# Hybrid encoder layer: the last layer norm taken during the last three expert units, their tokens normed apart

## Chip, cores and metric

The kernel runs on one core of a Trainium2 chip. The metric is device time in microseconds (us) of one execution, the median of several. Engines are named as the profile names them: PE (matrix products), DVE, ACT and POOL (elementwise work; POOL also issues transfers, among them all indirect ones), SP (issues transfers only). Sixteen DMA engines move the data of all issuing engines. Each engine runs its own instructions strictly in the order in which they stand.

## What is computed

A token-mixing sub-layer (sparse attention beside a convolution branch), then a mixture of experts, each with a residual and a layer norm. The change touches the end of the second sub-layer, for 512 prompt tokens and 64 sample tokens (576 rows of 1024 floats):

```
h2 = x * (1 + sc2) + sh2
# top-1 group, top-2 of its 4 experts: every token has two of 16 experts
act = silu(gate) * up * combine[:, :, None]
y = einsum('nef,efd->nd', act, w_down)
x = layer_norm(ALPHA * x + (1 + g2) * y, ln2_g, ln2_b)
```

## The kernel before

The first 690 us or so are the dense part: modulation products (`adap`, weights `wada`), the input projection (`acc`, weights split into a high and a low part by ACT L139 and DVE L140), attention, convolution, output projection, first norm, routing. A scheduler orders this part by its own timing model. The first modulation products need `wada` loads from SP's queue; `hh` and `hl`, the inputs of every `acc` product, need those.

Two rows of DRAM scratch stand for each token in `z_scr`: rows 0 to 575 begin as the residual, rows 576 to 1151 as a broadcast row (L416, one 2304 KB copy from DRAM to DRAM that POOL issues; L418 does the same for `h2_scr`). A token's first expert adds its result to the token's first row, the second expert to its second row, so z = row t + row 576 + t is what the last norm takes.

The experts run in thirteen units, an order written out by hand on PE, DVE and ACT (`manual_schedule`). Units 0 to 3 are four fixed experts; units 4, 8, 10 and 12 hold one expert with up to 128 tokens; units 5 and 6 one expert in two blocks; units 7, 9 and 11 two small experts with up to 64 tokens each. For each block POOL gathers the tokens' rows (L1119, `xg`), PE transposes them (L1134), multiplies by gate and up weights (`pg`), ACT and DVE make `hm`, PE turns it (`pht`) and ACT copies it (`hT`, L1166). The down product (`pd`; L1182, or L1186 for two experts) of one unit stands between the steps of the next unit: `product(p)` makes the row of gates `yo` on ACT and DVE (L1172, L1173), multiplies it with `pd` (L1193), and POOL adds the rows to `z_scr` (`add_rows`, L1194: an indirect transfer that accumulates, called a scatter below). Weights come into a ring of four slots through SP's queue; expert j's slot is free for expert j + 4, and the last weight loads are issued in the time of unit 9's product.

After the last unit all engines read a flag for overflowing experts (L1492, L1494); a loop would handle those and runs zero times here. The last unit's scatter is issued behind that. Then, for five tiles of 128 (the last 64) tokens: SP loads both rows of each token (`zt`, L1525), DVE adds them (L1527), tile 0 takes its statistics on DVE and the others on ACT (L1515, L1517, L1518), DVE applies them with gain and bias (`rows3`; L1529, L1530), and SP stores to y (L1531).

## Time and profile before

| what | value |
|---|---|
| median of 3 runs | 878.06 us (875.38 to 880.29) |
| the profiled execution | 880.75 us |
| its span (first to last instruction) | 879.1 us |
| PE, DVE, ACT, POOL busy | 90%, 74%, 41%, 15% of the span |
| clock granted to PE over the span | 0.95 of full |

The span is counted from the first instruction's time; the profiled execution's own time is 1.65 us longer than the span. A time such as "at 840.92" is microseconds from the span's start in the profiled execution. A row of the timeline gives start, duration, engine, line and operation, and in brackets how long the engine stood idle before it and what released it.

### The profile page before, as it was taken

How to read it: one execution, taken by the hardware profiler on the slowest of the kernel's cores; microseconds unless marked ns; L12 is line 12 of the kernel's file. 1: busy time of each engine (PE TensorE's matmuls, PEld its weight loads, DVE VectorE, ACT ScalarE, POOL GpSimd, SP SyncE). 2: the span in 40 equal slices, each digit the busy share in tenths (PEclk: the TensorE clock that was granted, in tenths of full speed). 3: DMA queues.
4: the chain of work that ended last, by engine and by line, in shares of the span. 5: the costliest groups of instructions: out<-in, count | busy, mean ns of one | idle time of the engine just before them, and what ended most of it. 6: DMA issues, size and time to landing. Idle time of an engine off the chain costs nothing.

```text
span 879.1 us, 13265 instructions
## 1 busy us (share of the span) xinstructions
PE 792.4 (90%) x4827; PEld 641.6 (73%) x4827; DVE 647.6 (74%) x1275; ACT 358.5 (41%) x654; POOL 132.3 (15%) x169
## 2 busy tenths in 40 slices
PE   4899999999999999999999999899938999999910
PEld 3788888887878879879899799888826676645400
DVE  1569999989999889988896425428896896655337
ACT  3243141324344335547733852312433664334304
POOL 2300000310100000000100001020347342221100
PEclk9999999999999999999999999899957999999965
DMA  9998663482423224232443106585695999699345
GB/s 295 343 340 261 195 213 119 122 241 54 149 71 95 76 75 113 89 100 84 129 118 113 39 1 228 188 259 213 197 329 139 345 366 310 199 363 373 97 164 169
DMA packets 101202, 162.06 MB, mean 184 GB/s; under 512 B 9667, under 2 KB 67163, under 8 KB 101137
## 3 DMA queue, kind: packets, MB, share of 16 engines
q1 hardware_dynamic: 87104, 122.74, 42.3%
q0 software_dynamic: 12688, 34.26, 14.5%
q10 hardware_dynamic: 1344, 4.22, 1.3%
q8 instruction: 38, 0.62, 0.3%
q14 instruction: 28, 0.22, 0.1%
HBM read 146.01 MB, written 26.13 MB: 196 GB/s over the span
## 4 chain that ended last, share of the span: by engine, by line
PE 60%; DVE 7%; DMA 4%; issue 2%; ACT 1%; POOL 1%; POOLq 0%; DVEq 0%; ACTq 0%
PE acc L242 7%; PE acc L244 7%; PE acc L243 7%; PE pd L1182 5%; PE pdot L528 3%; PE pg L1152 2%; PE pg L144 2%; DMA wraw<-in_w_att_out_dram 2%; PE pg L146 2%; PE pg L145 2%; PE tm L144 2%; PE tm L146 2%; PE tm L145 2%; PE pl L652 2%; PE po L660 2%
## 5 line engine op out<-in xcount | busy, mean ns | idle before, releaser
L588 DVE SCALAR_TENSOR_TENSOR y<-ue,dwT,y 128x604 f32<-128x604 f32 (+17 forms) x232 | 183.3, 828 | 1.9 <-ACT y L586 1.6
L242 PE MATMUL acc<-hh,wlo 128*128 128x288 f32 (+1 forms) x504 | 152.9, 304 | 1.3 <-DVE wlo L140 1.3
L243 PE MATMUL acc<-hh,whi 128*128 128x288 f32 (+1 forms) x504 | 150.6, 299 | 0.0
L244 PE MATMUL acc<-hl,whi 128*128 128x288 f32 (+1 forms) x504 | 149.4, 300 | 0.0
L139 ACT CAST whi<-wraw 128x1024 fp32r<-128x1024 f32 (+1 forms) x72 | 75.1, 1044 | 175.2 <-PE acc L244 83.1
L140 DVE TENSOR_TENSOR wlo<-wraw,whi 128x1024 fp32r<-128x1024 f32 (+1 forms) x72 | 87.4, 1214 | 53.6 <-ACT whi L139 53.3
L242 PEld LDWEIGHTS acc<-hh,wlo 128*128 128x128 f32 (+1 forms) x504 | 94.4, 187 | 17.2 <-issue 8.8
L243 PEld LDWEIGHTS acc<-hh,whi 128*128 128x128 f32 (+1 forms) x504 | 94.4, 187 | 5.2 <-issue 5.1
L244 PEld LDWEIGHTS acc<-hl,whi 128*128 128x128 f32 (+1 forms) x504 | 93.7, 187 | 5.5 <-issue 5.2
L144 PE MATMUL tm<-wlo,hh 128*128 128x512 f32 x128 | 50.5, 397 | 0.4 <-DVE wlo L140 0.4
L145 PE MATMUL tm<-whi,hh 128*128 128x512 f32 x128 | 50.4, 394 | 0.0
L146 PE MATMUL tm<-whi,hl 128*128 128x512 f32 x128 | 49.8, 391 | 0.0
L140 DVE TENSOR_TENSOR wlo<-ring,whi 128x1024 fp32r<-128x1024 f32 x30 | 36.4, 1222 | 17.7 <-ACT whi L139 15.0
L1182 PE MATMUL pd<-ring,hT 128*128 128x512 f32 x96 | 44.0, 601 | 1.2 <-ACT hT L1166 1.2
L139 ACT CAST whi<-ring 128x1024 fp32r<-128x1024 f32 x30 | 31.3, 1048 | 31.2 <-PE pg L146 27.4
L242 PE MATMUL acc<-oh,wlo 128*128 128x288 f32 x128 | 39.7, 310 | 4.5 <-DVE gt L744 4.0
L244 PE MATMUL acc<-yl,whi 128*128 128x288 f32 x128 | 39.3, 310 | 0.6 <-DVE yl L721 0.5
L244 PE MATMUL acc<-ol,whi 128*128 128x288 f32 x128 | 39.3, 310 | 0.0
L243 PE MATMUL acc<-oh,whi 128*128 128x288 f32 x128 | 39.2, 307 | 0.0
L243 PE MATMUL acc<-yh,whi 128*128 128x288 f32 x128 | 38.3, 301 | 0.0
L242 PE MATMUL acc<-yh,wlo 128*128 128x288 f32 x128 | 37.9, 297 | 0.0
L1194 POOL DMA_INDIRECT z_scr<-yo,idt x13 | 22.3, 1712 | 83.2 <-DVE yo L1193 74.4
(482 smaller groups left out, 1773.5 us busy)
## 6 DMA issues: line engine op xcount, KB each, us to landing
ring<-in_w_gate_up_dram SPq DMA_DIRECT2D x62, 512.0 KB
wraw<-in_w_in_dram SPq DMA_DIRECT2D x48, 512.0 KB
wada<-in_w_ada_dram SPq DMA_DIRECT2D x32, 512.0 KB
ring<-in_w_down_dram SPq DMA_DIRECT2D x32, 512.0 KB
wada<-in_w_ada_dram SPq DMA_DIRECT2D x32, 256.0 KB
gates_scr<-glg POOLq DMA_DIRECT2D x16, 288.0 KB
gt<-gates_scr POOLq DMA_DIRECT2D x16, 288.0 KB
wraw<-in_w_conv_out_dram SPq DMA_DIRECT2D x8, 512.0 KB
```

Of the source, the lines that this page charges most:

```text
L139: split_copy[0] = S.copy(hi, raw).ins
L140: V.tensor_tensor(lo, raw, hi, op=OP.subtract)
L144: PE.matmul(out, lh, rl, start=start, stop=False)
L145: PE.matmul(out, lh, rh, start=False, stop=False)
L146: PE.matmul(out, ll, rh, start=False, stop=stop)
L242: PE.matmul(ps[h][0:m, 0:288], wl[:, k, :], xh[:, k, sl], start=k == 0, stop=False)
L243: PE.matmul(ps[h][0:m, 0:288], wh[:, k, :], xh[:, k, sl], start=False, stop=False)
L244: return PE.matmul(ps[h][0:m, 0:288], wh[:, k, :], xl[:, k, sl], start=False, stop=k == KT - 1).ins
L528: PE.matmul(pdt[0:n, 0:L], qiT[pr, h // 2, 128 * t:128 * t + n], kiT[pr, k0:k0 + L], start=True, stop=True)
L588: V.scalar_tensor_tensor(y[:, 30 - i:EXT], ue[:, 0:EXT - 30 + i], dwT[:, j, i:i + 1], y[:, 30 - i:EXT], op0=OP.mult, op1=OP.add)
L1182: PE.matmul(pd_[c], hT[:, k, :], dns[0][k][:, cs], start=k == 0, stop=k == 1)
L1194: sc = G.indirect_dma_start(out=z_d, out_offset=bass.IndirectOffsetOnAxis(ap=ids[1], axis=0), in_=y, in_offset=None, bounds_check=2 * T - ...
```

## The change

Each output row begins as `ln2_b` (a copy from one DRAM row to all 576 rows of y, issued by POOL). When the sums of units 0 to 9 stand in `z_scr`, SP loads all five tiles (`tile_rows`, ten loads), and their norm is taken between the steps of units 11 and 12: DVE sums the two rows with an accumulated row sum (`summed`), ACT squares (`measured`), root and reciprocal follow (`scales`), ACT scales, DVE multiplies by the gain, and POOL adds the tile to y (`tile_done`, an accumulating store). These norms lack units 10, 11 and 12. So for each of these three units POOL gathers both `z_scr` rows of the unit's tokens after the unit's scatter (`unit_rows`), they are normed apart (`unit_done`), and two indirect stores, one for prompt and one for sample rows, write them over what stands in y (`unit_store`). For unit 12 its own result is added from `yo` in place of a second read. The loop for overflowing experts norms everything again if it runs.

```diff
+    for s, n in enumerate((SEQ, DEC)):
+        G.dma_start(dap(o["y"][s], 0, [[D, n], [1, D]]), dap(a["ln2_b"], 0, [[0, n], [1, D]]))
     G.dma_start(dap(z_d, T * D, [[D, T], [1, D]]), dap(rows_d, 9 * D, [[0, T], [1, D]]))
...
+    def tile_rows(t):
+        z12[t] = [xg[(nb + i) % 3][0:DEC] for i in range(2)] if t == 4 else [piece(*x) for x in both_rows(t)]
+        for i, z in enumerate(z12[t]):
+            last_rows[0] = SY.dma_start(z, dap(z_d, (i * T + t * 128) * D, [[D, TS[t]], [1, D]])).ins
...
+    def unit_rows(i):
+        e = plan[DEFER + i][0]
+        z12[NT + i] = [piece(*x) for x in both_rows(NT + i)]
+        z_gather(z12[NT + i][1], other[:, e:e + 1])
+        z_gather(z12[NT + i][0], idt[:, 1, e:e + 1])
+
+    def summed(t, to=None):
+        z, n = z12[t][0], z12[t][0].shape[0]
+        V.scalar_tensor_tensor(z, z, 1.0, z12[t][1] if to is None else to, op0=OP.mult, op1=OP.add,
+                               accum_out=st2[0:n, 0, t:t + 1])
+        V.tensor_scalar(st2[0:n, 0, t:t + 1], st2[0:n, 0, t:t + 1], -1.0 / D, None, op0=OP.mult)
...
+    def tile_done(t):
+        z, n = z12[t][0], TS[t]
+        S.activation(z, z, AF.Identity, bias=st2[0:n, 3, t:t + 1], scale=st2[0:n, 2, t:t + 1])
+        V.tensor_tensor(z, z, rows3[0][0:n], op=OP.mult)
+        with tc.issue_after(last_rows[1]):
+            G.dma_start(dap(o["y"][t // 4], (t % 4) * 128 * D, [[D, n], [1, D]]), z, accum_op=OP.add)
+
+    def unit_done(i):
+        z, t, e = z12[NT + i][0], NT + i, plan[DEFER + i][0]
+        V.scalar_tensor_tensor(z, z, st2[:, 0, t:t + 1], rows3[0], op0=OP.add, op1=OP.mult)
+        V.scalar_tensor_tensor(z, z, st2[:, 2, t:t + 1], rows3[1], op0=OP.mult, op1=OP.add)
+
+    def unit_store(i):
+        z, e = z12[NT + i][0], plan[DEFER + i][0]
+        for s, (idx, n) in enumerate(((idt[:, 0, e:e + 1], SEQ), (sample[:, e:e + 1], DEC))):
+            G.indirect_dma_start(out=dap(o["y"][s], 0, [[D, n], [1, D]]), out_offset=bass.IndirectOffsetOnAxis(ap=idx, axis=0),
+                                 in_=z, in_offset=None, bounds_check=n - 1, oob_is_err=False)
...
+        L3 = DEFER
+        aside = {("p", L3 - 1): [do(tile_rows, 0), do(tile_rows, 1)],
+                 (L3 + 1, 0): [do(tile_rows, 2)],
+                 (L3 + 1, 1): [do(tile_rows, 3)],
+                 ("r", L3 + 1): [do(tile_rows, 4)],
+                 ("p", L3): [rows3_loads],
+                 (L3 + 1, 2): [do(unit_rows, 0)],
+                 (L3 + 1, 3): [do(summed, 0), do(measured, 0), do(summed, 1)],
+                 ("r", L3 + 2): [do(measured, 1)],
+                 ("p", L3 + 1): [do(unit_rows, 2), do(unit_rows, 1), do(scales, 0, 2), silu_back, do(tile_done, 0),
+                                 do(summed, 2)],
+                 (L3 + 2, 2): [do(summed, 3)],
+                 (L3 + 2, 3): [do(tile_done, 1), do(summed, 4)]}
...
-        for i in range(len(pend)):
-            turn_next(i)
-            product_next(i)
+        p = pend[0]
+        turn_next(0)
+        p.y = gate_row(p.ar[2], p.ar[3])
+        p.pd = down(p.hT, p.dns)
+        measured(2)
+        summed(NT)
+        measured(NT)
+        scales(2, 3)
+        add_rows(p.y, p.pd, p.ar[0])
+        V.tensor_tensor(z12[NT + 2][0], z12[NT + 2][0], z12[NT + 2][1], op=OP.add)
+        summed(NT + 2, p.y)
+        tile_done(2)
...
+        for i in range(1, 3):
+            unit_done(i)
+            unit_store(i)
...
-    for t in range(NT):
-        n, s = TS[t], int(t == 4)
-        z2 = slot([128, 2, D], name="zt")
-        SY.dma_start(z2[0:n], dap(z_d, t * 128 * D, [[D, n], [T * D, 2], [1, D]]))
```

In the table `aside`, ("p", u) stands behind the product of unit u, (u, c) behind step c of unit u, ("r", u) behind the transposes that follow step 1 of unit u; `DEFER` is 10. Line numbers of the changed kernel are two higher than before from L418 on (L1194 is L1196, L1119 is L1121).

Two engines' programs show where this lands. First POOL at the very start of the program: `dwr`, `stc`, `rq` and `ri` are small inputs, `arow` a scratch tile whose clearing waits for PE. Before:

```order
L249 DMA dwr<-in_w_dw_dram 31x512
L250 DMA stc<-in_state_conv_dram 30x512
L349 DMA rq<-in_rope_q_dram 128x320
L350 DMA ri<-in_rope_i_dram 128x160
L345 MEMSET arow 128x3072
L374 DMA arow<-in_b_ada_dram 2x512
```

In the changed kernel:

```order
L249 DMA dwr<-in_w_dw_dram 31x512
L250 DMA stc<-in_state_conv_dram 30x512
L349 DMA rq<-in_rope_q_dram 128x320
L350 DMA ri<-in_rope_i_dram 128x160
L417 DMA out_dram<-in_ln_b_dram 512x1024
L417 DMA out_dram<-in_ln_b_dram 64x1024
L345 MEMSET arow 128x3072
L374 DMA arow<-in_b_ada_dram 2x512
```

The scheduler has put the two copies that fill y (2304 KB together) among the first transfers of the program, ahead of the instruction at which POOL waits for PE; in the text they stand behind the modulation.

Second, POOL from the last scatter before unit 10's to the end of the tile and unit stores. Before, where `yo` of units 9, 10 and 11, the flag `ovi`, and behind the flag's branch the scatter of unit 12 follow one another (units 9 to 11 are the last three of a row of five scatters):

```order
L1119 DMA xg<-h_scr,idt 128x1024
L1194 DMA z_scr<-yo,idt 1152x1024 x5
L1492 TENSOR_LOAD ovi
L1494 COMPARE_AND_BRANCH
L1494 ISA
```

In the changed kernel, with numbers so that the tiles can be told apart (`yo_7874` is unit 10's, `yo_7935` unit 11's, `yo_8001` unit 12's; `other` and `idt` are the indices of a token's other and own row; each two `L1332` are the gathers of unit 10, of unit 12 and of unit 11):

```order
L1196 DMA z_scr<-yo_7874,idt_6466 1152x1024
L1332 DMA ring_6574<-z_scr,other_6570 128x1024
L1332 DMA ring_6555<-z_scr,idt_6466 128x1024
L1196 DMA z_scr<-yo_7935,idt_6466 1152x1024
L1332 DMA ring_6575<-z_scr,other_6570 128x1024
L1332 DMA ring_6575<-z_scr,idt_6466 128x1024
L1374 DMA out_0_dram<-ring_6545 128x1024 x2
L1196 DMA z_scr<-yo_8001,idt_6466 1152x1024
L1374 DMA out_0_dram<-ring_6550 128x1024 x2
L1374 DMA out_1_dram<-xg_6539 64x1024
L1384 DMA out_0_dram<-ring_6555,idt_6466 512x1024
L1384 DMA out_1_dram<-ring_6555,sample_6571 64x1024
```

Between the scatters now stand gathers that read the rows which the scatter before them wrote, and which the scatter behind them writes; the stores to y (`L1374` adds a tile, `L1384` writes a unit's rows, twice more for units 11 and 12) follow on the same engine, all ahead of the flag.

## Rows read from the trace of the kernel before

**Rows 1.** Page, the span in 40 slices: PE busy and DMA share in tenths.
```profile
PE   4899999999999999999999999899938999999910
DMA  9998663482423224232443106585695999699345
```

**Rows 2.** Busy time by stretch, first 60 us (columns named in the first line).
```profile
core 0: us, PE busy (x) PEld busy (x) DVE busy (x) ACT busy (x) POOL busy (x), PEclk, DMA share, GB/s
5.10:17.70 12.60, 7.20 (x44) 5.62 (x44) 1.67 (x5) 5.60 (x9) 0.00 (x0) 1.00 1.07 327
17.70:28.40 10.70, 7.13 (x130) 4.20 (x129) 4.09 (x8) 1.83 (x3) 6.70 (x9) 0.94 1.12 332
28.40:60.00 31.60, 30.22 (x315) 28.22 (x313) 17.53 (x39) 12.52 (x23) 2.89 (x6) 0.97 1.07 365
```

**Rows 3.** Timeline of PE where the modulation ends and the input projection begins.
```profile
27.43 1.07 PE L219 MATMUL adap<-wada,cT 128*32 128x128 f32 x12 [0.38 <-DMA wada<-in_w_ada_dram]
28.42 0.61 PE L242 MATMUL acc<-hh,wlo 128*128 128x288 f32 x1
```

**Rows 4.** Timeline of POOL: the start, and copies from DRAM to DRAM.
```profile
4.49 0.58 POOL L350 DMA_DIRECT2D ri<-in_rope_i_dram  x1
20.88 2.66 POOL L345 MEMSET arow<- 128x3072 f32 x1 [15.81 <-PE adap L219]
...
182.19 1.15 POOL L418 DMA_DIRECT2D h_scr<-rows_scr  x2 [11.69 <-DMA rows_scr<-arow]
```

**Rows 5.** Busy time by stretch while the fill of `h2_scr` runs.
```profile
183.00:198.00 15.00, 15.00 (x74) 11.99 (x72) 14.05 (x30) 5.85 (x16) 1.70 (x3) 1.00 0.88 237
```

**Rows 6.** Busy time by stretch, the dense part behind the start.
```profile
60.00:640.00 580.00, 571.23 (x3608) 493.05 (x3607) 466.72 (x915) 238.69 (x474) 51.26 (x90) 0.99 0.46 138
```

**Rows 7.** Timeline of POOL: the scatters of units 9, 10 and 11.
```profile
809.28 1.55 POOL L1194 DMA_INDIRECT z_scr<-yo,idt  x1 [10.33 <-DVE yo L1193]
819.88 1.55 POOL L1194 DMA_INDIRECT z_scr<-yo,idt  x1 [9.05 <-DVE yo L1193]
830.54 1.55 POOL L1194 DMA_INDIRECT z_scr<-yo,idt  x1 [9.11 <-DVE yo L1193]
```

**Rows 8.** Chain of work that ended last: start, us, what.
```profile
840.92 6.11 DMA z_scr<-yo,idt
847.05 5.42 DMA zt<-z_scr
```

**Rows 9.** Busy time by stretch, around unit 9's scatter and in the old loads.
```profile
810.00:815.00 5.00, 5.00 (x28) 2.20 (x27) 2.84 (x3) 1.99 (x5) 0.83 (x1) 1.00 1.02 383
815.00:820.00 5.00, 5.00 (x18) 1.95 (x18) 3.86 (x5) 1.89 (x3) 0.12 (x1) 1.00 0.55 180
850.00:855.00 5.00, 0.00 (x0) 0.00 (x0) 2.48 (x3) 0.00 (x0) 0.00 (x0) 0.50 1.02 417
```

**Rows 10.** Timeline: three gathers of unit rows, and PE's first use.
```profile
659.75 3.23 POOL L1119 DMA_INDIRECT xg<-h_scr,idt  x1 [2.13 <-DVE fl L1207]
663.29 1.18 POOL L1119 DMA_INDIRECT xg<-h_scr,idt  x1 [0.30 <-issue]
...
666.10 1.12 PE L1134 MATMUL pxt<-ident,xg 128*128 128x128 f32 x4 [2.38 <-DMA xg<-h_scr,idt]
```

**Rows 11.** Timeline of the old norm: an add, a two-step operation, a small one, a square.
```profile
866.93 1.20 DVE L1527 TENSOR_TENSOR zt<-zt 64x1024 f32<-64x1024 f32 x1
...
873.53 0.15 DVE L1519 RECIPROCAL mv<-mv 64x1 f32<-64x1 f32 x1
873.71 1.28 DVE L1530 SCALAR_TENSOR_TENSOR zt<-zt,mv,rows 64x1024 f32<-64x1024 f32 x1
...
868.23 1.15 ACT L1517 ACTIVATE jk<-zt,mv 128x1024 f32<-128x1024 f32 x1 [1.24 <-DVE mv L1516]
```

**Rows 12.** Waits of SP's queue at the end: us in total, times, longest.
```profile
SPq L1572 <- DMA out_dram<-zt: 2.3, 1, 2.3
```

**Rows 13.** Timeline of ACT: unit 11's `hT` and unit 12's `hm`.
```profile
825.45 0.37 ACT L1166 COPY hT<-pht 128x256 f32<-128x256 f32 x1 [1.87 <-PE pht L1164]
...
832.51 0.38 ACT L1157 ACTIVATE hm<-pg 128x256 f32<-128x256 f32 x1 [5.64 <-PE pg L146]
```

More of the change, by code (lines that the diff above doesn't have):

```diff
@@ L1273, in place_ids, with other_rows @@
         return [idr, ido[:, 0:1]], ido.bitcast(F32)[:, 1:2], so[:, 0:1], so[:, 1:2]
+    other = late.tile([128, NE], I32, name="other", bufs=1)
+    sample = late.tile([128, NE], I32, name="sample", bufs=1)
+    def other_rows():
+        V.scalar_tensor_tensor(tok, idt[:, 0], 2.0, idt[:, 1], op0=OP.mult, op1=OP.subtract)
+        V.tensor_scalar(other, tok, float(T), None, op0=OP.add)
+        V.tensor_scalar(tok, idt[:, 0], float(SEQ), float(OOB), op0=OP.is_lt, op1=OP.mult)
+        V.scalar_tensor_tensor(sample, idt[:, 0], -float(SEQ), tok, op0=OP.add, op1=OP.add)
     def static_args(es):
@@ new lines, in scales, with silu_back, rows3_loads @@
+    def scales(t0, t1):
+        S.activation(st2[:, 2, t0:t1], st2[:, 1, t0:t1], AF.Sqrt, bias=epst, scale=1.0 / D)
+        V.reciprocal(st2[:, 2, t0:t1], st2[:, 2, t0:t1])
+        V.tensor_tensor(st2[:, 3, t0:t1], st2[:, 0, t0:t1], st2[:, 2, t0:t1], op=OP.mult)
+    def silu_back():
+        S.activation(z12[0][1][:, 0:1], st2[:, 1, 0:1], AF.Silu)
+    rows3 = []
+    def rows3_loads():
+        rows3.extend(piece(16, 4 + i) for i in range(2))
+        with tc.issue_after(last_rows[0]):
+            brow(rows3[0], a["ln2_g"], 0, SY)
+            brow(rows3[1], a["ln2_b"], 0, SY)
```

71 lines of the change are left out of this document (52 added, 19 removed).

## The prediction

> **What bounds the kernel now.** I read the page's slices first, then busy time by stretch, then the chain of waits, then the timelines at both ends. Three stretches have three different limits. In the first 60 us the DMA engines are full: share 1.07, 1.12 and 1.07 [rows 2], and the slices show it too [rows 1]. PE ends its last modulation products on a `wada` load that has just landed and goes straight into the first `acc` product at 28.42 [rows 3]; so whatever delays SP's loads up to there delays all that follows. From 60 to 640 us PE is busy 571 of 580 us [rows 6]: a late start is not made up there. The end, from the last `pd` to 879.1, is a chain without PE: the scatter of unit 12 issued at 840.92 and landed 6.11 us later, first tile of `zt` 5.42 us after that [rows 8], then DVE and ACT by turns until 875, a store, the end. These 38 us from 840.92 are what the change goes for.
>
> **What the fill of y costs.** It is 2304 KB copied from DRAM to DRAM, as large as the two fills of `z_scr` and `h_scr`. It is not placed where those are: in POOL's order it stands directly behind `ri`, so it is issued at about 5.1 us [rows 4], ahead of the clearing at 20.88, and its data compete with `wada` while the DMA engines are full. Nothing hides it. Its price, from above: in 183 to 198, when the `h_scr` fill runs, 15 us at share 0.88 are 13.2 us of all engines, and 237 GB/s move 3.56 MB [rows 5]; 2.36 MB of these are the fill, the other 1.20 MB would take 3.3 us at the 365 GB/s of the start [rows 2]; left 9.9 us. From below: 2.36 MB at that full rate are 6.5 us. A gain is excluded, as nothing is taken away at the start. I take 9 us, near the upper end, as that row is the same kind of copy beside the same kind of load. PE waits for it once, before 28.4, and carries it to the end: **+9**.
>
> **Small additions.** `other_rows` is four DVE operations on 16 columns and the clearing of `st2` one; a small operation lasts 0.15 us in the old norm [rows 11]; with DVE idle between unit steps they cost nothing, 0.6 us without that cover.
>
> **What the end gains and loses.** Removed is the old tail: loads, adds, statistics, stores, 847.05 to 879.1. In its place comes a chain on SP and POOL that starts earlier but is long, because every reader of `z_scr` waits for the writer before it and every writer for the readers. I follow it on the clock of the trace of before (the +9 comes on top).
>
> 1. SP's first `tile_rows` waits for unit 9's scatter, issued at 809.28 [rows 7]. With free DMA it would land 6.1 us later, 815.4 [rows 8]; the engines are at share 1.02 with the last weights until 815 and at 0.55 until 820 [rows 9]. I take 818 (815.4 to 820).
> 2. Ten tile loads, 4.72 MB, at 417 GB/s [rows 9]: 11.3 us; or 5.42 us for the first MB as before [rows 8] and 8.8 for the rest, 14.2. I take 13: all landed at 831.
> 3. Unit 10's scatter now waits for all ten loads, since it writes where they read. It was issued at 819.88; now at 831, landed 6.1 later at 837.1. POOL takes things in order, so all behind it wait too.
> 4. Two gathers of unit 10's rows wait for that landing. A gather takes 1.2 us to issue and 0.3 between; the first one of the kernel was in PE's hands 3.1 us after its issue ended (659.75 + 3.23 to 666.10) [rows 10]. 0.3 + 1.2 + 0.3 + 1.2 + 3.1 = 6.1: 843.2.
> 5. Unit 11's scatter, issued at 830.54 before, waits for these gathers: 843.5, landed 849.6.
> 6. Four gathers: the first pair is there at 849.6 + 6.1 = 855.7, the second 3.0 later.
> 7. DVE stands behind unit 12's add (1.2) until 855.7, then the sum with `yo` (1.3), tile 2's gain (1.2), unit 10's two operations (2.6), tile 3's gain (1.2), and six small ones (0.6): 863.8, by rows of the old norm [rows 11]. ACT's squares (1.15 each) lie beside it.
> 8. Tile 3's accumulating store: 0.6 to issue, 4.6 as a scatter takes behind its issue (6.11 - 1.55) [rows 7, 8], and 1 us in line behind the other tile stores and unit 12's scatter: 870. The stores of tiles 0 and 1 and unit 12's scatter are issued earlier, from 854 to 860, and lie beside steps 6 to 8.
> 9. The three prompt stores of the units go over the tiles and over each other, so each waits for the landing before it. A plain store was waited for 2.3 us at the end [rows 12], a scatter 4.6 behind its issue; with 0.3 + 1.2 to issue, each takes 3.8 to 6.1. I take 4.3: 870 + 12.9 = 883. The last sample store follows 1.2 later. Before, 4.1 us lie between DVE's last operation and 879.1, of them 0.5 for the store's issue and 2.3 for its landing, so 1.3 are left behind a landing: 885.5.
>
> So the end comes at 885.5 instead of 879.1: **+6.4**. From below, with each step at its shortest (815.4, 11.3, 3.8 per unit store, no line in step 8), it is about 877, -2; from above (820, 14.2, 6.1 per unit store, and the five accumulating stores one after another at 4.6), about 894, +15.
>
> Also moved: ACT now squares tile 0 and 1 and loads two tables around unit 11's `hT` (825.45) and before unit 12's `hm` (832.51) [rows 13]. Tile 0's sum and square (1.3 and 1.15) stand ahead of `hT`, tile 0's gain and two more sums (1.2 and 2.6) ahead of `hm` on DVE; so unit 12's product moves some 6 us, to about 845. That is hidden, as unit 12's `yo` is first needed in step 7 at 855.7; without that cover it would add its 6 us.
>
> **The sum.** 879.1 + 9 + 6.4 = 894.5 of span; with the 1.65 us around the span, 896.2 for an execution like the profiled one. That one (880.75) lies 2.7 above the median of 878.06, so I forecast **893.5** for the median.
>
> **A page beside it.** The landings of steps 3 to 9 are 3 to 6 us in the rows. The Trainium skill, page "DMA: Bandwidth & Descriptors", section "Anatomy of one DMA — SWDGE (gpsimd) path", puts a transfer issued from POOL at about 2.0 us plus bytes over 436 GB/s, thus at an estimated 3.2 us for a 512 KB scatter against the 6.11 measured. An estimate by that rule makes two scatters 2.9 us and the tile store 1.4 us shorter, and the sum about 886; the measured row decides for me, and the rule's result is the second rival.
>
> **Rivals.** First, the fill is hidden: if SP's loads come first on the engines and the fill trickles in behind 60 us, where the share falls [rows 2, 1], its cost is 0 and the time 884.5. Against it: in rows 5 the same copy takes most of the engines' time beside SP's loads. Chance 0.10. Second, short links: if the landings are like a plain store's, the end is at -2 and the time 885; for it speaks rows 12, against it rows 8 and 10. Chance 0.12. Third, slower stores: if five accumulating stores run one after another at 4.6 us, tile 3 lands near 880 and the time is some 903; the trace of before has no direct accumulating store. Chance 0.15. Fourth, on the other side, faster: the place is the waits on `z_scr` and y in steps 3, 5 and 9. If they do not bind, POOL's gathers and stores run as soon as their data are there, and the end hangs on unit 12's `yo` alone: its add at about 845, DVE's chain of step 7 (6.9 without the first add) 852, a store of 3.8 and the end (2.5) 858, or -21; with the +9 the time is 866. It decides where the chain of steps 2 to 9, 67 us from 818 to 885.5, is shorter by over 20 (6.4 + 9 + 4.4). Against it: POOL's order has the readers and writers of the same rows by turns. Chance 0.05. That the change does not do what it says, the tiles' norm being taken at the end as before, would show as the third case or worse.
>
> **How the numbers follow.** The forecast has 0.58. Between them the low cases (fill hidden, short links) lie at 884 to 885, the slow one at 903; with the fill's bounds (6.5 to 9.9) and those of the end, 883 to 904 leaves out some 2 in 10. About 0.5% (4.4 us) is what a measurement of this kernel can tell from no change: under 873.7 faster, over 882.4 slower. Faster 0.05; within, from the low tails of the first, second and fourth rival, 0.09; slower 0.86.
>
> **What would show it.** In the profile of the changed kernel: the first `acc` product near 37 instead of 28.4, with PE waiting for `wada`; unit 10's scatter issued some 20 us after where it stood (11 of it for the loads); gathers of unit 10, scatter of unit 11 and gathers of units 12 and 11 one behind the other on POOL; DVE idle some 8 us before the add of unit 12's rows; three prompt stores with 4 us between them at the end. It is wrong if the first `acc` product starts before 32, if unit 10's scatter is issued as soon as its `yo` is there, or if the stores to y land within a few us of each other.

## The result, and the profile after

The changed kernel takes **913.5 us** (median of 4 runs, 907.24 to 914.62) where the kernel before takes 877.64 on the same chip: a ratio of 1.039, 95% interval 1.034 to 1.045. The forecast was 893.5 with a range of 883 to 904, so the sign was right and the loss more than twice as large as forecast: 36 us where 15.4 stood. The profiled execution took 912.73 with a span of 911.1, so 32.0 of span are to be found. Of the 20 us by which the forecast fell short, 16.6 lie in this span (894.5 was forecast); the other 3.4 come from the step to the median: the forecast took 2.7 off, as the profiled execution of the kernel before lay that far above its median, and the one of the changed kernel lies 0.8 below its own.

Three landmarks divide the span. The first is GpSimd's first copy of modulation rows (line 412), which all PE work of the start stands ahead of. The second is the issue of unit 9's scatter [rows 7 has it before], which the change leaves alone. The third is the end.

| | before | after | more |
|---|---|---|---|
| start to first copy of L412 | 112.45 | 123.31 | +10.9 |
| from there to unit 9's scatter | 696.8 | 697.0 | +0.1 |
| from there to the end | 69.8 | 90.8 | +21.0 |

The middle part has no share in it. Over the kernels below it varies between 691.8 and 698.1 us without regard to what was changed, and that is also most of the spread of the medians; so small steps are read from the first and the last part of the traces, and the times stand beside them.

**The start.** Busy time by stretch (columns as in rows 2) and PE's timeline (start, us, engine, line, operation, what it waited for) of the changed kernel, and last PE's one wait for `xin` in the kernel before:

```profile
5.10:17.70 12.60, 5.61 (x25) 4.56 (x25) 1.66 (x5) 4.33 (x7) 1.07 (x2) 0.91 1.01 326
17.70:28.40 10.70, 4.54 (x48) 4.00 (x52) 0.00 (x0) 1.92 (x4) 0.00 (x0) 0.50 1.01 316
28.40:60.00 31.60, 28.83 (x370) 25.11 (x363) 17.89 (x42) 7.74 (x12) 8.69 (x13) 0.94 1.09 347
```
```profile
15.33 1.92 PE L263 MATMUL px<-ident,xin 128*128 128x128 f32 x8 [2.91 <-DMA xin<-in_x_prompt_dram]
23.86 1.94 PE L263 MATMUL px<-ident,xin 128*128 128x128 f32 x8 [6.62 <-DMA xin<-in_x_prompt_dram]
35.51 0.40 PE L242 MATMUL acc<-hh,wlo 128*128 128x288 f32 x1
```
```profile
15.74 1.06 PE L263 MATMUL px<-ident,xin 128*128 128x128 f32 x8 [1.03 <-DMA xin<-in_x_prompt_dram]
```

The fill is issued at 4.98, as forecast. The DMA engines are as full as before (1.01 against 1.12 in the second stretch, [rows 2]), but part of what they carry is the fill, and PE waits 9.5 us for two loads of `xin`, the prompt's tokens, where it waited 1.0 before. Its waits for `wada` up to the first `acc` product fall from 2.8 us to 1.4 meanwhile, and this product comes 7.1 us later than in rows 3, as the two differences have it (8.5 less 1.4). Of the granted clock, which in rows 2 is 1.00 and 0.94 in the first two stretches, 0.91 and 0.50 are left while PE waits (0.50 is the lower of its two levels); in the third stretch PE is busy 1.4 us less than before. By line 412 the 7.1 have become 10.9; where these 3.8 are lost is not shown here.

**The tail.** Timeline of the changed kernel on GpSimd (POOL), SyncE's queue (SPq) and DVE, from unit 9's scatter on:

```profile
820.26 1.57 POOL L1196 DMA_INDIRECT z_scr<-yo,idt  x1 [10.31 <-DVE yo L1195]
829.65 4.88 SPq L1329 DMA_DIRECT2D ring<-z_scr  x8
834.70 1.21 SPq L1329 DMA_DIRECT2D xg<-z_scr  x2
836.94 0.34 SPq L756 DMA_DIRECT2D ring<-in_ln_g_dram  x1
848.09 1.57 POOL L1196 DMA_INDIRECT z_scr<-yo,idt  x1 [26.26 <-SPq L1627]
848.19 1.23 DVE L1372 TENSOR_TENSOR ring<-ring 128x1024 f32<-128x1024 f32 x1 [3.21 <-SPq L1627]
854.83 1.06 POOL L1332 DMA_INDIRECT ring<-z_scr,other  x1 [5.17 <-ACT yo L1174]
861.26 1.23 DVE L1344 SCALAR_TENSOR_TENSOR ring<-ring 128x1024 f32<-128x1024 f32 x1 [5.10 <-DMA ring<-z_scr,idt]
861.96 2.02 POOL L1196 DMA_INDIRECT z_scr<-yo,idt  x1 [4.74 <-DMA ring<-z_scr,idt]
865.87 1.28 DVE L1195 TENSOR_TENSOR yo<-yo,pd 128x512 f32<-128x512 f32 x2
867.95 1.03 POOL L1332 DMA_INDIRECT ring<-z_scr,other  x1 [3.97 <-issue]
873.97 1.23 DVE L1605 TENSOR_TENSOR ring<-ring 128x1024 f32<-128x1024 f32 x1 [6.82 <-DMA ring<-z_scr,idt]
882.26 0.86 POOL L1374 DMA_DIRECT2D out_dram<-ring  x1 [2.08 <-DVE st L1356]
891.29 1.38 POOL L1384 DMA_INDIRECT out_dram<-ring,idt  x1 [5.39 <-DMA out_dram<-ring]
896.88 0.98 POOL L1384 DMA_INDIRECT out_dram<-ring,idt  x1 [2.87 <-DMA out_dram<-ring,idt]
900.28 0.97 POOL L1384 DMA_INDIRECT out_dram<-ring,idt  x1 [1.15 <-issue]
901.56 0.98 POOL L1384 DMA_INDIRECT out_dram<-ring,sample  x1 [0.30 <-issue]
```

The name in the brackets is that of the last release which the profile saw, and where an engine waits for several things it need not be the one that counts (SPq L1627, at unit 10's scatter and at DVE's row behind it, is the branch of the loop for overflowing experts, which stands behind both). What a step waits for is therefore read from the order of the program and from the runs below. The steps of the forecast can be read one by one: tile loads, unit 10's scatter (848.09), its gathers (854.83), unit 11's scatter (861.96), four gathers (867.95), the add of unit 12's rows (873.97), tile 3's accumulating store (882.26), three prompt stores (891.29, 896.88, 900.28). The rows of busy time behind them show an end that nothing fills:

```profile
903.00:906.00 3.00, 0.00 (x0) 0.00 (x0) 0.00 (x0) 0.00 (x0) 0.00 (x0) 0.50 0.05 11
906.00:911.10 5.10, 0.00 (x0) 0.00 (x0) 0.00 (x0) 0.00 (x0) 0.00 (x0) 0.50 0.00 0
```

Counted from unit 9's scatter, in the forecast and as measured:

| step | forecast | measured | more |
|---|---|---|---|
| scatter 9 to first tile load | 8.7 | 9.4 | 0.7 |
| first load to unit 10's scatter (ten loads landed) | 13.0 | 18.4 | 5.4 |
| that scatter to DVE's sum of its gathered rows | 12.2 | 13.2 | 1.0 |
| to unit 11's scatter | 0.3 | 0.7 | 0.4 |
| to the add of unit 12's rows | 12.2 | 12.0 | -0.2 |
| to tile 3's store | 8.1 | 8.3 | 0.2 |
| tile 3's store to the first prompt store | 6.2 | 9.0 | 2.8 |
| first to third prompt store | 8.6 | 9.0 | 0.4 |
| third prompt store to the end | 6.9 | 10.8 | 3.9 |
| sum | 76.2 | 90.8 | 14.6 |

So the chain is the one forecast, and three of its links were too short: the loads, the accumulating store, the end. The experiments ask for each whether it is what it seems, what the fill is made of, and whether the turns on `z_scr` are what binds.

### The profile page after: what moved, and what is told of

Its sections match the earlier page's. It is cut to its first block, busy times and chain, and to the rows that moved or that the text cites. A ratio compares the mean times of both kernels' runs of the same rounds, so it can differ in the third digit from the quotient of the medians.

```text
span 911.1 us, 13363 instructions
## 1 busy us (share of the span) xinstructions
PE 797.3 (88%) x4827; PEld 645.5 (71%) x4827; DVE 653.3 (72%) x1301; ACT 367.6 (40%) x663; POOL 151.6 (17%) x188
## 5 line engine op out<-in xcount | busy, mean ns | idle before, releaser
L1184 PE MATMUL pd<-ring,hT 128*128 128x512 f32 x96 | 47.2, 638 | 0.9 <-ACT hT L1168 0.9
L712 POOL DMA_DIRECT2D gates_scr<-glg x16 | 8.7, 542 | 171.6 <-ACT glg L711 96.2
```

What stands on the lines that cost most here:

```text
L712: G.dma_start(gates_d[m], sg)
L1184: PE.matmul(pd_[c], hT[:, k, :], dns[0][k][:, cs], start=k == 0, stop=k == 1)
```

## The experiments

All numbers in one place; times in us. The tail is read from unit 9's scatter (U9) and from unit 10's (U10), in one trace of each kernel.

| kernel | ratio to before (95%) | first L412 | U9 to U10 | U10 to the end | U9 to the end |
|---|---|---|---|---|---|
| before | 1 | 112.45 | 10.6 | 59.2 | 69.8 |
| changed | 1.039 (1.034 to 1.045) | 123.31 | 27.8 | 63.0 | 90.8 |
| no_fill | 1.024 (1.016 to 1.032) | 112.32 | 28.0 | 63.3 | 91.3 |
| late_fill | 1.027 (1.021 to 1.033) | 112.45 | 28.0 | 63.4 | 91.5 |
| spread_fill | 1.030 (1.023 to 1.038) | 121.79 | 28.7 | 63.7 | 92.4 |
| rows_early | 1.032 (1.025 to 1.038) | 121.92 | 28.4 | 64.2 | 92.6 |
| no_rows | 1.032 (1.027 to 1.036) | 121.77 | 27.5 | 64.1 | 91.5 |
| no_tile4 | 1.032 (1.027 to 1.036) | 122.34 | 23.8 | 64.8 | 88.6 |
| plain_stores | 1.035 (1.029 to 1.040) | 121.55 | 29.7 | 58.8 | 88.5 |
| units_apart | 1.030 (1.025 to 1.036) | 123.94 | 29.7 | 55.8 | 85.6 |
| no_loop | 1.034 (1.031 to 1.037) | 122.03 | 28.8 | 60.3 | 89.1 |
| own_scratch | 1.032 (1.025 to 1.039) | 124.06 | 10.6 | 76.8 | 87.4 |
| own_no_rows | 1.021 (1.017 to 1.025) | 123.27 | 10.6 | 67.0 | 77.6 |
| pool_end | 1.003 (1.001 to 1.006) | 112.43 | 10.6 | 60.4 | 71.0 |
| split_norm | 1.008 (1.006 to 1.011) | 112.69 | 10.6 | 63.8 | 74.4 |
| accum_tiles | 1.006 (1.003 to 1.008) | 113.01 | 10.6 | 62.3 | 72.9 |

In the seven kernels that leave the tile loads alone (changed, the three on the fill, plain_stores, units_apart, no_loop) the way from U9 to U10 lies between 27.8 and 29.7, so what a later step gains is read from U10 on. In the seven that leave alone all that stands behind the loads (changed, the three on the fill, rows_early, no_rows, no_tile4) the way from U10 to the end lies between 63.0 and 64.8, so of a step that is read there less than 2 us can't be told from none.

### The fill: left out, moved, and from other rows

First the two copies are left out (no_fill):

```diff
-    for s, n in enumerate((SEQ, DEC)):
-        G.dma_start(dap(o["y"][s], 0, [[D, n], [1, D]]), dap(a["ln2_b"], 0, [[0, n], [1, D]]))
```

then they are issued among GpSimd's stores of keys and values instead, behind `stored`, which turned out to be at 231 us (late_fill):

```diff
+    with tc.issue_after(stored): [G.dma_start(dap(o["y"][s], 0, [[D, n], [1, D]]), dap(a["ln2_b"], 0, [[0, n], [1, D]])) for s, n in enumerate((SEQ, DEC))]
```

and at the old place they read other rows (spread_fill):

```diff
-        G.dma_start(dap(o["y"][s], 0, [[D, n], [1, D]]), dap(a["ln2_b"], 0, [[0, n], [1, D]]))
+        G.dma_start(dap(o["y"][s], 0, [[D, n], [1, D]]), dap(a[("x_prompt", "x_sample")[s]], 0, [[D, n], [1, D]]))
```

> The changed kernel without its two fill copies (rows of y that no unit store writes then lack the bias). It asks what the fill costs in all. In the changed kernel the first acc product stands 7.1 us later than before (35.51 against 28.42), and unit 9's scatter 11.0 us later (820.26 against 809.28). Theory A, the fill is the whole shift: unit 9's scatter back at 809 to 810, time 902 to 903 us (11 less than 913.5). Rival B, the fill is only the shift of the first product and the other 4 us come from later instructions of the change: scatter at 813 to 814, time 906 to 907.

> The changed kernel with the fill issued among GpSimd's stores of keys at about 240 us, where the DMA engines are busy for 20 to 40 per cent of the slices. Theory: hidden there, so the time is that of the kernel without the fill within 1 us (902 to 903), unit 9's scatter at 809 to 811. Rival: the same bytes hold up the stores of keys and the gate rows behind them, and 4 us or more of the 11 come back (906 or more).

> The changed kernel with the fill at its old place, but copied from x (576 different rows) and not from the one row of ln2_b; y then holds x in place of the bias. Between 842 and 847 the changed kernel's loads of ln2_g and ln2_b, one row read for 128 partitions, ran at 143 to 232 GB/s with the DMA engines full, where the loads of z ran at 400 and more. Theory: it is the reading of one row that makes the fill dear, so half of the 11 us goes: first acc product near 32, time 907 to 909. Rival: a copy from DRAM to DRAM costs this whatever it reads: 35.5 and 912 to 914 as in the changed kernel.

Medians: 903.3, 902.8 and 907.14 us. GpSimd's timeline at the first copy of line 412, in the changed kernel:

```profile
123.31 1.00 POOL L412 DMA_DIRECT2D rows_scr<-arow  x2 [56.03 <-DVE arow L401]
```

without the fill:

```profile
112.32 1.00 POOL L412 DMA_DIRECT2D rows_scr<-arow  x2 [53.75 <-DVE arow L401]
```

with the late fill:

```profile
112.45 1.01 POOL L412 DMA_DIRECT2D rows_scr<-arow  x2 [53.74 <-DVE arow L401]
```

and with the fill from other rows:

```profile
121.79 1.01 POOL L412 DMA_DIRECT2D rows_scr<-arow  x2 [56.01 <-DVE arow L401]
```

The fill is the whole delay of the start. Without it, or with it at 231 us, the copy is issued where it was before. Among the nine kernels with the plain fill at the start it lies between 121.55 and 124.06, among the six without between 112.32 and 113.01: the fill costs 8.5 to 11.7 us there, and nothing that shows at 231 us. Theory A and that of late_fill hold (902 to 903 expected). The theory of spread_fill fell: with 576 different rows the copy stands at 121.79, among the others. Its lower median says nothing for it: no_rows, with the plain fill, has the same 907.14. The wrong guess came from the slow stretch at 842 to 847; what that was, no_rows and no_tile4 show.

### What holds unit 10's scatter for 18 us

The loads of `ln2_g` and `ln2_b` ahead of the tile loads (rows_early; unit 10's weights are later written over them, so the rows are scaled by other numbers):

```diff
-        aside = {("p", L3 - 1): [do(tile_rows, 0), do(tile_rows, 1)],
+        aside = {("p", L3 - 1): [rows3_loads, do(tile_rows, 0), do(tile_rows, 1)],
...
-                 ("p", L3): [rows3_loads],
```

these loads left out (no_rows):

```diff
-        rows3.extend(piece(16, 4 + i) for i in range(2))
-        with tc.issue_after(last_rows[0]):
-            brow(rows3[0], a["ln2_g"], 0, SY)
-            brow(rows3[1], a["ln2_b"], 0, SY)
+        rows3.extend((gr0, gr1))
```

and the last tile's loads left out (no_tile4):

```diff
-        for i, z in enumerate(z12[t]):
+        for i, z in enumerate(z12[t] if t < 4 else ()):
```

> The changed kernel with the loads of ln2_g and ln2_b ahead of the ten tile loads on SyncE's queue in place of behind them. In the changed kernel the ten loads took 18.2 us from the first issue (829.65) to the last landing (unit 10's scatter at 848.09), where 13 had been forecast, and the engines ran slowly between 842 and 847. Theory: the two one-row loads stand in the way of the last tile loads; unit 10's scatter moves to about 844 and the time falls by 3 to 5 us, to 909. Rival: the two loads now delay the weights of units 11 and 12 by as much, and the time stays at 912 to 915.

> The changed kernel without its late loads of ln2_g and ln2_b (two gate rows that lie ready take their place, so the outputs are scaled by the wrong rows). With the loads placed early, unit 10's scatter stood 28.4 us behind unit 9's, as against 27.8 in the changed kernel. Theory: the ten tile loads alone hold it, so it stays 27 to 28 us behind, and the time falls by 1 us or less, to 912 to 913.5. Rival: the two loads share the DMA engines with the last tile loads and hold them up: 24 to 25 us behind, time down by 3 to 4, to 909 to 910.

> The changed kernel without the two loads of the last tile (64 rows each; its rows are then wrong). In the changed kernel they were issued last (834.70) and landed 11.4 us later, when unit 10's scatter was let go at 848.09. Theory: these two, slow and last in line, make the 18 us where 13 had been forecast: unit 10's scatter 23 to 25 us behind unit 9's in place of 27.8, and the time 3 to 4 us less, 909 to 911. Rival: the eight large loads land as late: 27 to 28 us behind, 912 to 914.

Medians: 908.2, 907.14 and 907.49 us. GpSimd's scatters of units 9 and 10 without the two rows:

```profile
814.07 1.57 POOL L1196 DMA_INDIRECT z_scr<-yo,idt  x1 [10.31 <-DVE yo L1195]
841.53 1.57 POOL L1196 DMA_INDIRECT z_scr<-yo,idt  x1 [25.89 <-DVE st L1356]
```

and without the last tile's loads:

```profile
820.47 1.57 POOL L1196 DMA_INDIRECT z_scr<-yo,idt  x1 [10.32 <-DVE yo L1195]
844.31 1.57 POOL L1196 DMA_INDIRECT z_scr<-yo,idt  x1 [22.28 <-DMA ring<-in_ln_g_dram]
```

The two rows don't hold the scatter: away it stands 27.5 behind unit 9's, ahead 28.4, against 27.8; the theory of no_rows holds and that of rows_early fell. Without the last tile's two loads it stands 23.8 behind, 4.0 sooner, as the theory of no_tile4 had it. (The load of `ln2_g` that the profile names there is none of the scatter's inputs, and without it, in no_rows, the scatter goes hardly sooner.) The medians, 907 to 908 us, don't tell these theories apart; spread_fill, with all of the loads, lies there too. Busy time by stretch at the end of the loads tells how, in the changed kernel:

```profile
835.00:842.00 7.00, 4.66 (x24) 1.95 (x22) 3.50 (x7) 3.77 (x6) 0.00 (x0) 1.00 1.00 406
842.00:847.00 5.00, 3.34 (x14) 2.17 (x12) 2.80 (x5) 4.94 (x8) 0.00 (x0) 1.00 1.04 231
```

without the two rows, when only the last tile's loads are left:

```profile
836.50:838.00 1.50, 1.50 (x6) 0.42 (x4) 1.15 (x1) 1.48 (x2) 0.00 (x0) 0.50 0.94 178
```

without the last tile's loads:

```profile
840.00:844.50 4.50, 4.50 (x23) 2.21 (x18) 2.33 (x3) 4.45 (x6) 0.19 (x1) 1.00 1.03 417
```

and in the kernel before, at the end of its own loads:

```profile
859.00:862.00 3.00, 0.00 (x0) 0.00 (x0) 1.69 (x5) 1.53 (x3) 0.00 (x0) 0.50 1.06 179
```

With the 64-row loads in line the engines are full (share 1.04) and carry 231 GB/s; with these loads alone they carry 178, and without them, the two row loads still there, 417. The two loads are 512 KB, some 1.3 us at that rate, and the forecast had these bytes in its sum; so of the 4.0 us about 2.7 are the price of the shape, an estimate from these two numbers. The kernel before has such a dip where its 64-row tile comes last, with stores to y beside it. There DVE was still at work on earlier tiles; here a scatter waits for the last byte. The end came 2.2 us sooner, not 4.0: from U10 on this kernel took 1.8 more.

### The store to y and the end

The tile stores plain (plain_stores):

```diff
-            G.dma_start(dap(o["y"][t // 4], (t % 4) * 128 * D, [[D, n], [1, D]]), z, accum_op=OP.add)
+            G.dma_start(dap(o["y"][t // 4], (t % 4) * 128 * D, [[D, n], [1, D]]), z)
```

the units' stores to arrays of their own (units_apart):

```diff
-            G.indirect_dma_start(out=dap(o["y"][s], 0, [[D, n], [1, D]]), out_offset=bass.IndirectOffsetOnAxis(ap=idx, axis=0),
+            G.indirect_dma_start(out=dap(u_d[i][s], 0, [[D, n], [1, D]]), out_offset=bass.IndirectOffsetOnAxis(ap=idx, axis=0),
```

the loop of lines 1625 to 1655 left out (no_loop), and, on the kernel before, its last store on GpSimd (pool_end):

```diff
-        SY.dma_start(dap(o["y"][s], (t % 4) * 128 * D, [[D, n], [1, D]]), zt[0:n])
+        (G if t == 4 else SY).dma_start(dap(o["y"][s], (t % 4) * 128 * D, [[D, n], [1, D]]), zt[0:n])
```

> The changed kernel with the five tile stores plain in place of accumulating (these rows then lack the bias). In the changed kernel tile 3's store took 9.0 us from its issue to the first unit store, with the DMA engines full between 880 and 889 at 170 GB/s. Theory: accumulating halves the rate, and plain stores are 3 to 5 us quicker there: time 908 to 911. Rival: the unit stores then wait for their own norms, 1 us less at most: 912 to 914.

> The changed kernel with the six stores of the last three units written to scratch arrays of their own in place of y, so that they wait neither for the tile stores nor for each other (y then keeps the tiles' rows for these tokens). In the changed kernel the first waits 5.4 us for the tile stores and the third is issued 9.0 us after the first. Theory: the order of writes to y is the price: the last store is issued about 8 us sooner (near 893 in place of 901.6), time 904 to 906. Rival: GpSimd's six issues and the norms of the units (2.6 us each on DVE) bind next: 4 us less, 909 to 910.

> The changed kernel without the loop over overflowing experts at its end, which this data never enters. In the changed kernel 9.5 us lie between the issue of the last unit store (901.56) and the end (911.1), where the forecast had about 2.5; with the last store of the kernel before on GpSimd it was 5.4. Theory: leaving the loop waits for the stores to land, and GpSimd closes its queue only after that; without the loop the close runs beside the landing, so 5 to 6 us lie there and the time is 909 to 910. Rival: six indirect stores take longer to close than one plain one, whatever stands between: 9 us again, 912 to 914.

> The kernel before, with the store of its last tile (64 rows) issued by GpSimd in place of SyncE. In the changed kernel 5 us lie idle behind the last landing, which the kernel before does not show. Theory: a GpSimd queue that has just moved data takes about 5 us to close at the program's end: 4 to 6 us more than before, 882 to 884. Rival: the idle end belongs to the leaving of the loop, which the changed kernel has behind its last stores: then within 1 us of before, 877 to 879.

Medians: 909.76, 907.35, 908.91 and 882.34 us (before beside the last: 879.73). GpSimd's timeline with plain stores, tile 3's and the first of a unit:

```profile
879.47 0.55 POOL L1374 DMA_DIRECT2D out_dram<-ring  x1 [2.37 <-DVE st L1356]
...
884.14 1.89 POOL L1384 DMA_INDIRECT out_dram<-ring,idt  x1 [1.32 <-DMA out_dram<-ring]
```

with the units' stores apart, the second unit's first and the last:

```profile
891.98 1.85 POOL L1384 DMA_INDIRECT u_scr<-ring,idt  x1 [3.35 <-DVE ring L1379]
...
896.74 0.98 POOL L1384 DMA_INDIRECT u_scr<-ring,sample  x1 [0.30 <-issue]
```

without the loop, the last:

```profile
897.53 0.98 POOL L1384 DMA_INDIRECT out_dram<-ring,sample  x1 [0.30 <-issue]
```

and in the kernel before with its last store on GpSimd:

```profile
869.81 0.61 POOL L1531 DMA_DIRECT2D out_dram<-zt  x1 [32.42 <-DVE zt L1530]
```

A plain tile store lets the first unit store go 4.7 us behind its issue, an accumulating one 9.0, so accumulating costs 4.3 there, and from U10 on the kernel is 4.2 shorter: the theory (3 to 5) holds. (The 9.0 are not one store's alone: tile 2's, issued 3.5 us earlier, and tile 4's are on the engines with it.) With the units' stores apart it is 7.2 shorter; the last store is issued 46.4 us behind U10 in place of 53.5, 7.1 sooner, near the theory's 8. DVE's norm of the second unit is what its store waits for then (3.35 us), which the rival had in mind, but it takes less than that expected; the median, 907.35, lies between the two.

Behind the last store's issue lie 9.5 us in the changed kernel (9.2 to 9.5 in the ten others that keep the loop there), 6.9 without the loop (904.4 - 897.53), and 5.4 with one plain store behind the old norm (875.2 - 869.81). Leaving the loop is 2.6 of it, and the 6.9 lie between what theory (5 to 6) and rival (9) of no_loop expected. That GpSimd's queue takes long to close is borne out only in part: pool_end's median is 2.6 us above before (0.4 to 5.1 by the interval of the ratio), less than the 4 to 6 expected, its tail 1.2 longer. What the 1.5 us between 6.9 and 5.4 are isn't settled. The expectation of no_loop sets "about 2.5" against the 9.5, which counts from the third prompt store's landing; from the last issue, as here, the forecast had about 5.6.

### Are the turns on z_scr what binds?

Units 10 to 12 scatter into a second scratch (own_scratch), and the same with the two rows left out as in no_rows (own_no_rows):

```diff
-            add_rows(p.y, p.pd, p.ar[0])
+            add_rows(p.y, p.pd, p.ar[0], z3_d if p.u >= DEFER else z_d)
```

> The changed kernel with units 10, 11 and 12 scattering into a second scratch, so that no scatter waits for a tile load or a gather, nor a gather for these scatters (their rows are then missing from the gathered sums). Theory, the turns of reading and writing the one scratch set the end: unit 10's scatter at about 845 in place of 848, its rows summed on DVE near 856 in place of 861, the last gathers landed before unit 12's product, whole time 12 to 14 us less than the changed kernel, 900 to 902. Rival, DVE's row of work is the bound, since unit 12's hm stands behind two tiles' sums: then the gathers only wait in another place, 2 to 4 us less, 910 to 911.

> Units 10 to 12 scatter into a second scratch, and the loads of ln2_g and ln2_b are left out too (gate rows take their place). With the second scratch alone DVE stood 12.8 us before tile 0's product with ln2_g, whose load landed 23.5 us after its issue beside the gathers, so the turns of reading and writing were not tried by themselves. Theory: taken away together, the tail from unit 9's scatter to the end falls from 90.8 us to 76 to 79, time 899 to 902. Rival, DVE's own row of work bounds the tail: 86 to 88 us, 909 to 911, as with the second scratch alone.

As the gathers no longer depend on unit 11's scatter, GpSimd's order is another too: all six stand ahead of that scatter. Medians: 909.54 and 895.97 us. The first kernel gave 3.4 us of tail and no more, near its rival, but not for the rival's reason. Its timeline has the reason, SyncE's load of `ln2_g` and DVE's first use of it:

```profile
838.28 0.34 SPq L756 DMA_DIRECT2D ring<-in_ln_g_dram  x1
...
861.77 1.22 DVE L1372 TENSOR_TENSOR ring<-ring 128x1024 f32<-128x1024 f32 x1 [12.78 <-SPq L1627]
```

With the gathers let loose the load of one row for all partitions was waited for until 23.5 us after its issue (11.3 in the changed kernel), and everything on DVE stood behind it, unit 12's `hm` too. That it is the gathers which hold this load up is likely, but was not tried by itself. In the changed kernel the same wait lies beside the turns (3.21 at 848.19). With both taken away the tail falls from 91.5 us (no_rows alone) to 77.6, as the theory had it; the time, 895.97, is below the 899 to 902 expected, as the middle part of this trace is 4.9 shorter than the changed kernel's. The scatters of units 9 and 12, DVE between them, and the last store on its GpSimd:

```profile
815.28 1.56 POOL L1196 DMA_INDIRECT z_scr<-yo,idt  x1 [10.31 <-DVE yo L1195]
...
858.31 1.28 DVE L1195 TENSOR_TENSOR yo<-yo,pd 128x512 f32<-128x512 f32 x2
859.51 1.22 DVE L1605 TENSOR_TENSOR ring<-ring 128x1024 f32<-128x1024 f32 x1
859.87 2.33 POOL L1196 DMA_INDIRECT z_scr<-yo,idt  x1 [7.58 <-DVE yo L1195]
...
883.37 0.98 POOL L1384 DMA_INDIRECT out_dram<-ring,sample  x1 [0.30 <-issue]
```

So the turns cost 13.9 us, and a second limit, the landing of `ln2_g`, stood close behind them: undoing either alone gave little. Even without both the tail is 7.8 us longer than before (69.8). What is left stands ahead of unit 12's product, not behind it. Its last operation in the kernel before:

```profile
838.16 0.69 DVE L1193 TENSOR_TENSOR yo<-yo,pd 128x512 f32<-128x512 f32 x1 [0.63 <-PE pd L1182]
```

Unit 12's `yo` is finished 29.6 us behind U9 there, and 44.3 in own_no_rows, 14.7 later, where the tiles' sums and scalings stand ahead of `hm` and of this product on DVE and ACT. The add of unit 12's rows (859.51) follows it at once. From `yo` to the end it is 40.2 us before and 33.3 here, 6.9 less: the early norm does shorten the end, but it delays the last unit by twice as much.

### The cheap parts without the turns

The kernel before with its last norm written in another way, per tile (split_norm):

```diff
+        V.scalar_tensor_tensor(zt, zt, 1.0, z2s[t][0:n, 1, :], op0=OP.mult, op1=OP.add, accum_out=sn[0:n, 0, t:t + 1])
...
+        S.activation(zt, zt, AF.Identity, bias=sn[0:n, 3, t:t + 1], scale=sn[0:n, 2, t:t + 1])
+        V.tensor_tensor(zt, zt, rows3[0:n, 0], op=OP.mult)
+        (V if t == NT - 1 else G).tensor_tensor(zt, zt, rows3[0:n, 1], op=OP.add)
```

and with stores that accumulate on a filled y in place of GpSimd's additions (accum_tiles):

```diff
-        (V if t == NT - 1 else G).tensor_tensor(zt, zt, rows3[0:n, 1], op=OP.add)
+        if s:
+            V.tensor_tensor(zt, zt, rows3[0:n, 1], op=OP.add)
+        out = dap(o["y"][s], (t % 4) * 128 * D, [[D, n], [1, D]])
+        SY.dma_start(out, zt) if s else G.dma_start(out, zt, accum_op=OP.add)
```

> The kernel before, tail and all, with only its last norm written another way: the sum's total taken by DVE's addition itself, scaling by ACT, the bias added by GpSimd (by DVE for the last tile), no rows apart and no fill. Before, DVE is busy for 3.9 of 4 us between 866 and 870 with about 4.1 us a tile; here it has 3.0 a tile, ACT 2.9, GpSimd 2.4 to 2.7, and the loads land 2.5 us apart. Theory: the tail is then bound by the loads and the last tile's chain: 4 to 6 us less than before, 873 to 876. Rival: GpSimd and DVE slow each other down on the same rows, or the order of the stores holds the last: within 1.5 us of before.

> The kernel before with the change's two cheap parts and none of its turns: the prompt's rows of y filled with the bias at about 240 us, the last norm's total taken by DVE's addition and its scaling by ACT, and tiles 0 to 3 stored accumulating by GpSimd, the last tile with DVE's own addition of the bias and a plain store by SyncE. DVE has about 3.0 us a tile in place of 4.1. Theory: the loads (2.5 us a tile) and the last tile's chain then bound the tail: 873 to 876, 3 to 5 less than before. Rival: the accumulating stores, at 170 GB/s as in the changed kernel, and the close of GpSimd's queue come out last: 877 to 881.

Neither beats the kernel before: 885.66 against 877.06 (0.6 to 1.1% slower) and 885.67 against 880.05 (0.3 to 0.8% slower). Timeline of split_norm, DVE and GpSimd: a small operation on a 128x1 tile by itself, and the same one beside GpSimd's addition:

```profile
854.58 0.16 DVE L1528 TENSOR_TENSOR sn<-sn 128x1 f32<-128x1 f32 x1
...
858.35 2.35 POOL L1531 TENSOR_TENSOR zt<-zt,rows 128x1024 f32<-128x1024 f32 x1 [18.24 <-DVE sn L1521]
858.37 2.34 DVE L1528 TENSOR_TENSOR sn<-sn 128x1 f32<-128x1 f32 x1
```

The work given to GpSimd came back on DVE as waiting, 2.2 us for one of its additions; the rival named this. DVE's last operation ends 70.3 us behind U9, as against 65.7 before, which is the 4.6 that the tail is longer; so the rival's time, within 1.5 us of before, was too good as well. In accum_tiles DVE is free of that, yet its last operation ends 65.9 us behind U9, as before (65.7): it now stands still for ACT's scaling. The last tile's plain store then goes out among accumulating ones that still fill the engines. Its timeline (DVE, SyncE) and busy time by stretch:

```profile
865.08 2.36 DVE L1530 TENSOR_TENSOR zt<-zt,rows 128x1024 f32<-128x1024 f32 x2 [2.18 <-ACT zt L1529]
...
871.49 0.53 SPq L1534 DMA_DIRECT2D out_dram<-zt  x1
```
```profile
870.00:873.00 3.00, 0.00 (x0) 0.00 (x0) 1.43 (x2) 0.00 (x0) 0.00 (x0) 0.50 1.06 193
```

The theory (DVE's work is what counts) fell. Of the 3.1 us that the tail is longer 2.8 lie behind DVE's last operation, where the rival put its two costs, the accumulating stores and the close of GpSimd's queue; which of them it is was not separated, and 885.67 is above the rival's 877 to 881. No version here is faster than the kernel before.

## Why the prediction was right or wrong

**Right.** The kind of loss, and both its places. The fill is issued where the order put it and can't be hidden there: +9 forecast (6.5 to 9.9), 8.5 to 11.7 over nine traces, 10.9 in the profiled one, which is over the upper end of 9.9, and all of it gone when it is moved to 231 us; the rival "fill hidden" is out. One detail was off: PE waited for `xin`, not `wada`, and the first `acc` product (37 forecast, 35.51 measured) shows only 7.1 of the 10.9; the rest was lost up to line 412. In the tail the readers and writers of `z_scr` take turns in just the order forecast, and own_no_rows shows that the turns cost 13.9 us once nothing stands beside them. So the rival "the waits don't bind" is out too, and so is "short links": of the nine steps only one came out shorter than forecast, by 0.2 us. The small additions cost nothing that shows (+0.1 between line 412 and U9).

**Wrong: the size of three terms of the tail,** 12.1 of the 14.6 us by which the tail is longer than forecast.

1. *Ten tile loads, 13 us (step 2).* They took 18.4. The bound from above, 14.2, went by the first tile's landing and the full rate, and both are rows of 128-row loads. The last two loads have 64 rows, and with them the engines carry 231 GB/s where they carried 406. no_tile4 gives 4.0 us back, of which some 2.7 are this shape and 1.3 bytes that step 2 had priced. The rest of the 5.4 was not tried by a run of its own; part of it is that the loads began at 324 GB/s (831 to 836) and reached the 417 of step 2 only then. The old tail hid the dip (179 GB/s at 859 to 862), so no step of the chain before showed it.
2. *Tile 3's accumulating store, 6.2 us (step 8).* It took 9.0 to the first unit store; plain stores take 4.7. The step took a scatter's landing and 1 us in line, and let the first tiles' stores lie beside; but the engines were full with them (183 GB/s at share 1.02 between 884 and 889, below). With plain stores the first unit store went 4.3 us sooner behind it. The third rival was this mechanism with too high a price.
3. *The end, 1.3 us behind a landing (step 9).* It was taken from a program that ends on SyncE behind a norm and has its loop ahead of unit 12's scatter, where leaving it shows as part of the 2.1 us between `yo` (done at 838.85) and the scatter (840.92). The change puts both the loop and GpSimd's stores last: from the third prompt store to the end 10.8 us in place of 6.9. That all the stores stand ahead of the flag and the loop could be seen in GpSimd's order, and step 9 put their leaving at nothing. no_loop gives 2.6 of the 3.9 us; of the other 1.3, pool_end's tail, 1.2 longer with a GpSimd store last, suggests that they belong to this store, but a difference that small is not shown by one trace.

The busy time of the changed kernel while the tile stores land:

```profile
884.00:889.00 5.00, 0.00 (x0) 0.00 (x0) 3.34 (x5) 2.28 (x5) 0.84 (x1) 0.50 1.02 183
```

**The links themselves** were sized well: scatter to gathers to sum 13.2 for 12.2, the second turn 12.0 for 12.2, DVE's row of operations 8.3 for 8.1, the prompt stores 9.0 for 8.6. The Trainium skill's rule, page "DMA: Bandwidth & Descriptors", section "Anatomy of one DMA — SWDGE (gpsimd) path", from which 3.2 us were estimated for a scatter, does not agree: 6.7 us lie between unit 10's scatter and the gather that waits for it (848.09, 854.83).

**The range** missed for the same reason: its upper end, 904, held the fill's and the stores' bounds, but the three terms were all short at once, and the end had no upper bound at all. Its sum also has a slip. The bound from above says that it holds the five accumulating stores one after another; yet the first load (2), the ten loads (1.2) and the unit stores (5.4) already make the 8.6 us from 885.5 to 894. The stores, which the third rival prices at some 10, are not in it. With them and the fill's 0.9 the upper end would have been near 913, close to the measured 913.5. (From below the terms named make 878.7, not 877.)

**A limit that was called hidden.** The forecast let DVE's tile work push unit 12's product by 6 us and saw no harm. In the changed kernel the product ends 17.3 us later behind U9 than before (at 867.15), but still ahead of the gathers that its add waits for (873.97), so the harm is hidden there; own_no_rows, where it comes 14.7 later, shows it. DVE also waited 3.2 us for `ln2_g` at 848.19, with unit 12's `hm` behind it, and in own_scratch this wait, 12.8 us, took nearly all that the turns gave back. The forecast spoke of no such wait: the loads of the two rows were not in its steps.

## What to carry to other kernels

A wait for many loads lasts until the one with the worst shape has landed: size the last one by a row of its own shape, not by the full rate. A transfer with no early reader belongs where the engines have room; the same 2304 KB cost some 10 us in the first 30 us, where they were full, and nothing that shows at 231, where their share was 0.3 to 0.4. When the last step of a program changes its queue, or a loop moves behind it, price the end anew; and before counting on the removal of a wait, look for the next one that stands beside it, and for the work that the change has put ahead of what remains.

## What was not expected of the hardware

- A two-input operation on DVE waits out a GpSimd addition: a 128x1 product on DVE took 0.16 us alone and 2.34 beside GpSimd's 2.35 us addition. The Trainium skill, page "SBUF — State Buffer", section "Who interferes with whom", says that a DVE instruction with two inputs in SBUF contends with a GpSimd instruction that reads SBUF, and that the port pair they share is an exclusive lock. The trace agrees: the product lasts as long as the addition beside it.
- Loads of a 64-row tile bring busy engines down to 178 GB/s (alone, share 0.94) and to 179 to 231 beside other transfers, where 128-row loads run at 406 to 417.
- A copy from DRAM to DRAM costs the same from 576 rows as from one (121.79 against 121.55 to 124.06 at the same landmark).
- Tile 3's accumulating store of 512 KB, with other tile stores on the engines, held the next one up for 9.0 us, a plain one in its place, among plain ones, for 4.7.
- 9.5 us lie between the last issue of a GpSimd store and the end of the program with a loop behind it that runs zero times, 6.9 without the loop.
